# Sums of down weights in DRAM at fixed places of each upper block, and no product of the modulation at the end of a head of the mixer

## The chip, the cores and the metric

The kernel runs on one core of one Trainium2 chip. The metric is the device time in microseconds (us). Everything is computed in one launch; weights and activations are f32 in DRAM, and the matrix products are made of pairs of fp32r numbers.

## What is computed (the reference, cut)

One layer of a residual block for 512 tokens of width 2048. A vector `c` gives six modulation vectors by one product with `w_ada` (12288 x 2048). The block has a mixer (a recurrent group and eight attention heads, both fed by one projection) and a gated feed-forward part of inner width 5632.

```python
mod = silu(c) @ w_ada[l] + b_ada[l]
sh1, sc1, gt1, sh2, sc2, gt2 = split(mod, 6)
h = rms_norm(x, g_mix) * (1 + sc1) + sh1
xr, yr, q, k, v, f_logit = split(h @ w_in, ...)
y_rec = rglru_group(xr, yr, ...)                    # conv, gates, scan, GeLU gate
y_att = forgetting_attention_group(q, k, v, f_logit, ...)   # 8 heads of 128
x = x + gt1 * (concat(rms_norm(y_rec), rms_norm(y_att)) @ w_out)
h2 = rms_norm(x, g_ffn) * (1 + sc2) + sh2
gate, up = split(h2 @ w_up, 2)
x = x + gt2 * ((silu(gate) * up) @ w_down)
```

## The kernel before

**How a product is made.** TensorE (PE) has no f32 product of full speed here, so each operand is split into a high part (ScalarE, ACT, a copy to fp32r) and a low part (VectorE, DVE, the difference), and each tile is multiplied three times: high by high, high by low, low by high (`mm`, L275). Weights are loaded from DRAM by DMAs that SyncE issues (SP queue), split by `wsplit` (L268; the tiles are called `...h` and `...l`), and there are three buffers of each. PE takes a half piece of weights (two k-steps) after another.

**The mixer.** For each head h, `tm_group` (L322) multiplies by the weights of the next head while `attention(h)` (L571) is worked off in hooks: small functions that are traced after a k-step n = 0 to 15 of that product. The statement `head_evac` (L560) copies a finished product out of PSUM at the start of a head, partly on DVE (L565), partly on ACT (L567, L568); the accumulators are used again by the next product. The softmax of a query block ends in a scaling on DVE (L633), then PE transposes (L639). Other hooks carry the recurrent group.

**The products of the modulation ("ada").** `ada_block` (L169) makes one block of 128 rows of `w_ada` times `c`: two DVE instructions on 128x1024 f32 (L178), each on a tile that a DMA brings (L166); the DMA of the next block is issued with the block before it. `ada1` (L509) makes one block; `H_ADA` (L49) says after which k-steps of which head one is made, and `WO_ADA` (L48) the same for the four column groups of the output projection, which come after the mixer. `behind` (L153) adds an order on DVE: not before the last instruction of a list (`norm_last`: the head's query and key normalisation, for steps up to 7; `soft_last`: the last softmax scaling, for later ones).

**The upper half of the feed-forward part.** After two ordinary groups come NBLK = 10 blocks b = 0 to 9. In each, a fast 2x2 scheme makes seven products instead of eight, in the order `ORDER` = 4, 5, 1, 7, 6, 2, 3 (L1145). A block loads four weight units U_A, U_C, U_B, U_D of 2 MB each in four DMAs (`load_unit`, L1150, L1163): U_A and U_C when product 4 is traced, U_B at product 1, U_D at product 2, all with a priority that puts them 2000 places ahead. Sums of units are made on DVE (`sum_unit`, L1168, L1170; two instructions a sum, on 128x2048): A+C for product 5, C+B for product 7, A+B for product 6, A+D for product 3. In between DVE makes pieces of the last modulation vector (`Gt2.piece`, L217, L222) from loads `gt` that SP issues in each block (`Gt2.loads`, L205, L211). Activations of the block before are transposed (`back`, L1196) and stored by eight DMAs `td` (L1088 to L1091).

**The sums of down weights in DRAM.** The lower half needs, for each of NQ = 11 parts q, a sum of three pieces of `w_down` (`s2d`) and of that with a fourth (`s4d`). `sums24(q, n)` makes them without an engine's arithmetic: step n = 0 copies two pieces DRAM to DRAM by four DMAs of 512 KB on the SP queue (L1105, L1106), behind the last weight load traced so far; steps 1 and 2 add two pieces to `s2d`, step 3 adds `s2d` to `s4d`, each by two accumulating DMAs of 512 KB on the queue of GpSimd (POOL, L1098).

```python
def dram_sum(out, src):
    for i in range(2):
        cs = slice(i * 1024, (i + 1) * 1024)
        nc.gpsimd.dma_start(out=out[:, cs], in_=src[:, cs], accum_op=ALU.add)
```

A product has eight k-steps j; after j = 3 and j = 7 a half is counted, so that a block has 14 halves. The counter `halves` runs through all ten blocks: with `SUMS_AT, SUMS_PER = 2, 12` a step n of a part comes every third half, and a new part every 12 halves, so that its place in the block moves from block to block.

**What sets the order.** A scheduler orders the instructions of each engine and queue ahead of time, by the place at which they are traced, by priorities and by `issue_after`; on the chip each engine and queue works its list off in that order and waits for semaphores. SP has the loads, the `td` stores and step 0 of the sums; POOL has in the upper half only the accumulating DMAs.

Of the kernel before, what the change touches and what calls it, by code (L numbers as in the profile page):

```python
# [44 lines left out]
T_STEPS = ((10, 11, 13, 15), (0, 4, 9, 15))  # L45
YR0_AHEAD = 80
CARRY = (0, 0, 1, 1, 1, 3, 3, 6)
WO_ADA = ((8, 10, 12, 14), (0, 3, 6, 9, 12), (0, 3, 6, 9, 12), (0, 3, 6, 9))  # L48
H_ADA = {1: (4, 7, 13, 15), 2: (4, 7, 13, 15), 3: (4, 7, 13, 15), 4: (4, 7, 13), 5: (4, 7, 13),  # L49
         6: (4, 7, 13, 15), 7: (1, 4, 7, 8, 10, 13)}  # L50
BIAS_STEPS = {0: (0, 0, 1, 1, 2, 2, 3, 3, 4, 4, 5, 5, 6, 6, 7, 7, 8, 8, 14, 15),
              1: (0, 0, 1, 1, 2, 2, 3, 3, 4, 4, 5, 5, 6, 6, 7, 7, 12, 13, 13, 14, 14, 14, 15, 15),
              2: (0, 0, 1, 1)}
# [7 lines left out]
KEEP = (2, 8, 2)  # L61
GT2_STEPS = ((4, 1), (4, 2), (4, 3), (4, 5), (4, 7), (5, 5), (6, 1))
GT2_N = (6, 6, 6, 6, 6, 6, 7, 7, 7, 7)
SUMS_AT, SUMS_PER = 2, 12
BU_PART = (0, 5, 10, 16)
BUP_STEP = 3
NQ = FT // 4
# [7 lines left out]
def block_kernel(ctx, tc, xT, crow, adaT, vecs, bfr, w1, wyr, wqkv0, wqkv, wgate, wout, wup0, wups, wdn, outT):  # L75
    nc = tc.nc
# [71 lines left out]
    mods = [cp.tile([P, KT], F32, name=f"mod{j}") for j in range(6)]  # L148

    ada_ready = {}  # L150
    soft_last, norm_last, gated = [], [], []

    def behind(f, gate):  # L153
        def g():
            gated[:] = gate
            f()
            gated.clear()
        return g
# [264 lines left out]
    for kt in range(KT):  # L423
# [12 lines left out]
        h, l = page(f"hph{kt}", "h"), page(f"hpl{kt}", "h")  # L436
# [16 lines left out]
    for f in (4, 5, 6, 7, 0, 1, 2, 3):  # L453
        t = page(f"xr{f}", "c")
# [32 lines left out]
    for kt in range(10):  # L487
        hk0.setdefault(max(RX_STEP, kt * 8 // 5), []).append(lambda kt=kt: sh1_block(kt))
    yr0 = fm_group(wyr[0], list(range(KT)), hp, "yr0", hooks=hk0, ahead=YR0_AHEAD,
                   ps=[misc(f"yr0p{f}") for f in range(3)] + [rgp("yr0p3")])  # L490
    rstd_x = rx[0]
    yr = []
    for f in range(4):
        t = page(f"yr{f}", "c")
# [10 lines left out]
    def add(hooks, n, *fns):  # L505
        hooks.setdefault(n, []).extend(fns)
        return hooks
# [52 lines left out]
    def head_evac(h, ps):  # L560
        qk = qp.tile([P, NT, 2 * P], F32, tag="qk", name=f"qk{h}")
        v = page(f"v{h}", "d", [P, NT, P])
        for t in range(NT):
            if t % 2:
                nc.vector.tensor_copy(out=qk[:, t, :], in_=ps[t][:, 0:256])  # L565
            else:
                nc.scalar.activation(qk[:, t, :], ps[t][:, 0:256], AF.Copy)  # L567
            nc.scalar.activation(v[:, t, :], ps[t][:, 256:384], AF.Copy)  # L568
        return qk[:, :, 0:P], qk[:, :, P:2 * P], v
# [266 lines left out]
    ps = tm_group(wqkv0, hs_, "h0", 392, hooks=hk0)  # L836
    frest = None
    for h in range(NH):
        with tc.high_priority(offset=EVAC):
            ev = head_evac(h, ps)  # L840
        if h == 0:
            frest = forget(ps)
            make_spn()
            conv_sums()
        att = attention(h, *ev)
        att[0]()
        hk = {}
        for n, f in zip(CARRY, carry):
            add(hk, n, f)
        carry = []  # L850
        if h == 0:
            for n, f in zip(FORGET_STEPS, frest):
                add(hk, n, f)
        for n, f in zip((FIRST_STEPS if h == 0 else ATT_STEPS if h < NH - 1 else LAST_STEPS)[1:], att[1:]):
            add(hk, n, f)
        for n in BIAS_STEPS.get(h, ()):
            f = lambda: bias_in(len(bias_done))
            add(hk, n, behind(f, soft_last) if h or n > 11 else f)
        if h == 2:
            add(hk, 2, bias_sum)  # L860
        if 2 <= h < 6:
            rp = rec_pair((2 * h - 4, 2 * h - 3))
            for n, f in zip(REC_STEPS, rp):
                add(hk, n, f)
            carry = rp[len(REC_STEPS):]
        for n in H_ADA.get(h, ()):
            add(hk, n, behind(ada1, soft_last if n > 7 else norm_last) if h < 7 else ada1)
        if h < NH - 1:
            ps = tm_group(wqkv[h], hs_, f"h{h + 1}", 384, hooks=hk)
    att_rms = cp.tile([P, NT], F32, name="att_rms")  # L870
# [119 lines left out]
    for g in range(4):  # L990
        hk = {}
# [15 lines left out]
        for f in range(4):  # L1007
            kt = g * 4 + f
            t = page(f"x1_{kt}", "c")
# [90 lines left out]
    def sums24(q, n):  # L1100
        if n == 0:
            with tc.issue_after((up_loads or stream_loads)[-1]):
                for i in range(2):
                    cs = slice(i * 1024, (i + 1) * 1024)
                    nc.sync.dma_start(out=s2d[q][:, cs], in_=wdn[0, q, :, cs])  # L1105
                    nc.sync.dma_start(out=s4d[q][:, cs], in_=wdn[1, q, :, cs])  # L1106
        elif n < 3:
            dram_sum(s2d[q], wdn[n + 1, q])
        else:
            dram_sum(s4d[q], s2d[q])  # L1110
# [11 lines left out]
    for gi in range(STD):  # L1122
        hk = {}
# [80 lines left out]

    gt2_left = [(r, i) for r in range(4) for i in range(KT)]
    hk = {}
    nprod = halves = 0
    for b in range(NBLK):
        un, keep_ = {}, {}
        gt2 = Gt2(gt2_left[:GT2_N[b]])  # L1210
# [4 lines left out]
        for i, p in enumerate(ORDER):  # L1215
# [3 lines left out]
            for j, hi, lo in prod_weights(p, b, un):  # L1219
                th, tl = T[p][j]  # L1220
                for t in range(2):
                    c_ = slice(t * P, (t + 1) * P)
                    mm(ps[t], th[:, c_], hi, j == 0, False)
                    mm(ps[t], th[:, c_], lo, False, False)
                    mm(ps[t], tl[:, c_], hi, False, j == 7)
                for fn in hk.get((i, j), ()):
                    fn()
                if j % 4 == 3:
                    n = halves - SUMS_AT
                    halves += 1  # L1230
                    if 0 <= n < SUMS_PER * NQ and n % SUMS_PER % 3 == 0 and n % SUMS_PER < 12:
                        sums24(n // SUMS_PER, n % SUMS_PER // 3)
            if b + i == 0:
                up_last()
            if p in (4, 5, 1, 7):
# [259 lines left out]
```

## Time and profile before

| | us |
|---|---|
| median of 3 runs | 2028.64 |
| lowest and highest of them | 2025.68, 2032.72 |
| the profiled execution, its own time | 2028.19 |
| its span in the profile | 2026.5 |
| PE busy, of that span | 2005.5 |
| DVE busy | 1678.2 |
| ACT busy | 986.8 |

The page gives, for each engine, the time in which it has an instruction at work, and for each group of instructions the idle time before it and what ended that idle time (the releaser). A stretch (window) gives the same for a part of the span, with the clock granted to PE as a share of full speed and the mean busy share of the 16 DMA engines; a share a little over 1 comes from rounding. Times in the text are us from the start of the span; "into the block" means from the first matmul of product 4 of that block. The ten blocks begin at 813.7, 889.8, 968.0, 1046.4, 1131.7, 1209.8, 1288.0, 1366.1, 1444.2 and 1522.4.

### The profile page before, as it was taken

What the parts mean: (1) busy time and instruction counts of PE and PEld (TensorE: products, weight loads), DVE (VectorE), ACT (ScalarE), POOL (GpSimd) and SP (SyncE); (2) the same over time, 40 slices, a digit from 0 to 9 for tenths busy, and PEclk for the clock granted to TensorE, in tenths of its full rate; (3) what the DMA queues carried; (4) which work ended last, traced back from release to release, by engine and by line L of the source; (5) the groups of instructions that cost most, each with busy time, mean ns of one, the idle gap of its engine ahead of it and who ended that gap; (6) DMA issues with size and microseconds to landing.
All of it is one profiled execution on the core that took longest, in us unless ns stands there. A gap on an engine that the chain in (4) does not pass through costs nothing.

```text
span 2026.5 us, 25606 instructions
## 1 busy us (share of the span) xinstructions
PE 2005.5 (99%) x9330; PEld 1688.7 (83%) x9330; DVE 1678.2 (83%) x2300; ACT 986.8 (49%) x1362; POOL 109.8 (5%) x138
## 2 busy tenths in 40 slices
PE   9999999999999999999999999999999999999999
PEld 7889988898888888888887888888888888888887
DVE  8999788877787769898797888988988977777786
ACT  4433446775422257544544544445445455445443
POOL 0000100111000000000010000000000100000000
PEclk9999999999999999999999999999999999999999
DMA  9989866557679874779698868878696677778793
GB/s 354 346 296 336 281 213 209 199 170 258 225 256 319 327 259 143 184 201 270 187 280 236 207 235 228 208 261 238 187 289 186 222 249 245 253 239 295 257 331 119
DMA packets 173683, 496.33 MB, mean 245 GB/s; under 512 B 18434, under 2 KB 41138, under 8 KB 169459
## 3 DMA queue, kind: packets, MB, share of 16 engines
q1 hardware_dynamic: 162372, 454.99, 65.4%
q0 software_dynamic: 11040, 39.59, 11.2%
q8 instruction: 73, 1.20, 0.2%
q14 instruction: 54, 0.44, 0.1%
q10 hardware_dynamic: 144, 0.11, 0.0%
HBM read 458.93 MB, written 93.36 MB: 273 GB/s over the span
## 4 chain that ended last, share of the span: by engine, by line
PE 87%; DVE 6%; issue 4%; DMA 2%; ACT 1%; POOL 0%; DVEq 0%; POOLq 0%; ACTq 0%
PE up_2p L276 5%; PE up_6p L276 5%; PE up_3p L276 5%; PE up_5p L276 5%; PE up_1p L276 5%; PE up_7p L276 5%; PE up_4p L276 5%; PE w1p L276 4%; PE dn4p L276 3%; PE dn6p L276 3%; PE dn3p L276 3%; PE dn1p L276 3%; PE dn2p L276 3%; PE dn7p L276 3%; PE dn5p L276 3%
## 5 line engine op out<-in xcount | busy, mean ns | idle before, releaser
L1170 DVE TENSOR_TENSOR uw<-uw,uw 128x2048 f32<-128x2048 f32 x80 | 182.5, 2282 | 2.0 <-DMA uw<-in_wups 2.0
L178 DVE SCALAR_TENSOR_TENSOR ada<-ada,c_b 128x1024 f32<-128x1024 f32 x96 | 116.7, 1221 | 46.3 <-DMA ada<-in_adaT 46.1
L271 ACT ACTIVATE up_1h<-uw 128x1024 fp32r<-128x1024 f32 x70 | 74.4, 1063 | 118.9 <-PE up_6p L276 21.6
L271 ACT ACTIVATE up_0h<-uw 128x1024 fp32r<-128x1024 f32 x70 | 74.3, 1062 | 115.0 <-PE up_4p L276 16.6
L272 DVE TENSOR_TENSOR up_1l<-uw,up_1h 128x1024 fp32r<-128x1024 f32 x70 | 85.3, 1219 | 36.1 <-ACT up_1h L271 36.1
L272 DVE TENSOR_TENSOR up_0l<-uw,up_0h 128x1024 fp32r<-128x1024 f32 x70 | 85.4, 1220 | 33.6 <-ACT up_0h L271 33.5
L271 ACT ACTIVATE up_3h<-uw 128x1024 fp32r<-128x1024 f32 x70 | 74.4, 1063 | 71.7 <-PE up_2p L276 14.9
L271 ACT ACTIVATE up_2h<-uw 128x1024 fp32r<-128x1024 f32 x70 | 74.2, 1060 | 58.4 <-PE up_2p L276 16.5
L272 DVE TENSOR_TENSOR up_2l<-uw,up_2h 128x1024 fp32r<-128x1024 f32 x70 | 85.3, 1218 | 20.0 <-ACT up_2h L271 19.9
L272 DVE TENSOR_TENSOR up_3l<-uw,up_3h 128x1024 fp32r<-128x1024 f32 x70 | 85.2, 1217 | 10.3 <-ACT up_3h L271 10.3
L1098 POOL DMA_DIRECT2D s2d<-in_wdn x44 | 36.5, 842 | 624.2 <-DMA s2d<-in_wdn 624.2
L276 PE MATMUL w1p<-hph,w1l 128*128 128x512 f32 x128 | 49.8, 389 | 0.0
L276 PE MATMUL w1p<-hpl,w1h 128*128 128x512 f32 x128 | 49.8, 389 | 0.0
L222 DVE SCALAR_TENSOR_TENSOR gt<-gt,gt_None 128x512 f32<-128x512 f32 x64 | 43.0, 683 | 5.5 <-DMA gt<-in_adaT 5.5
L276 PE MATMUL w1p<-hph,w1h 128*128 128x512 f32 x128 | 42.6, 392 | 0.0
L188 DVE SCALAR_TENSOR_TENSOR ada<-ada,c_b 128x1024 f32<-128x1024 f32 x32 | 39.0, 1218 | 4.0 <-DMA ada<-in_adaT 4.0
L188 DVE SCALAR_TENSOR_TENSOR adf<-adf,c_b 128x1024 f32<-128x1024 f32 x32 | 39.0, 1219 | 0.3 <-DMA adf<-in_adaT 0.3
L631 ACT ACTIVATE bt<-bt,nm 128x128 f32<-128x128 f32 (+3 forms) x32 | 17.9, 561 | 34.8 <-DVE nm L629 34.5
L712 DVE SCALAR_TENSOR_TENSOR ba<-bw,sh,ba 128x512 f32<-128x512 f32 x45 | 32.2, 743 | 0.0
L616 POOL TENSOR_SCALAR_AFFINE_SELECT bt<-bt 128x128 f32<-128x128 f32 x32 | 22.8, 735 | 116.2 <-ACT bt L615 116.2
L437 ACT ACTIVATE hph<-x,A 128x512 fp32r<-128x512 f32 x16 | 11.6, 723 | 35.0 <-DVE A L434 35.0
L276 PEld LDWEIGHTS w1p<-hph,w1h 128*128 128x128 f32 x128 | 24.0, 188 | 5.4 <-issue 0.6
(2293 smaller groups left out, 6637.8 us busy)
## 6 DMA issues: line engine op xcount, KB each, us to landing
uw<-in_wups SPq DMA_DIRECT2D x160, 512.0 KB, 7.2
ada<-in_adaT SPq DMA_DIRECT2D x128, 512.0 KB, 5.4
s2d<-in_wdn POOLq DMA_DIRECT2D x44, 512.0 KB, 8.8
adf<-in_adaT SPq DMA_DIRECT2D x32, 512.0 KB, 6.0
gt<-in_adaT SPq DMA_DIRECT2D x64, 256.0 KB, 6.1
s2d<-in_wdn SPq DMA_DIRECT2D x22, 512.0 KB, 8.9
s4d<-in_wdn SPq DMA_DIRECT2D x22, 512.0 KB, 9.9
s4d<-s2d POOLq DMA_DIRECT2D x22, 512.0 KB, 8.2
```

Source lines behind the costliest of these rows:

```text
L178: nc.vector.scalar_tensor_tensor(out=t, in0=t, scalar=1.0, in1=cs, op0=ALU.mult, op1=ALU.mult, accum_out=ac)
L188: nc.vector.scalar_tensor_tensor(out=t, in0=t, scalar=1.0, in1=c_b[:, cs], op0=ALU.mult, op1=ALU.mult, accum_out=ada_acc[j][:, hf, i:i + 1])
L222: nc.vector.scalar_tensor_tensor(out=t, in0=t, scalar=1.0, in1=c, op0=ALU.mult, op1=ALU.mult, accum_out=gt2_acc[:, r, i:i + 1])
L271: tail_hi.append(nc.scalar.activation(R(hi[:, :n]), raw_ap, AF.Copy).ins)
L272: tail_lo.append(nc.vector.tensor_sub(R(lo[:, :n]), raw_ap, hi[:, :n]).ins)
L276: nc.tensor.matmul(ps, lhsT=R(l), rhs=R(r), start=start, stop=stop)
L437: nc.scalar.activation(R(h), xt, AF.Copy, scale=a)
L616: nc.gpsimd.affine_select(out=bt[:, b * P:n], in_=bt[:, b * P:n], pattern=[[-1, P]], compare_op=ALU.is_ge, fill=NEG, base=0, channel_multi ...
L631: nc.scalar.activation(p[:, :n], p[:, :n], AF.Exp, scale=-1.0, bias=nm, accum_out=sm)
L712: nc.vector.scalar_tensor_tensor(out=ba[j], in0=src, scalar=s1, in1=ba[j], op0=ALU.mult, op1=ALU.add)
L1098: nc.gpsimd.dma_start(out=out[:, cs], in_=src[:, cs], accum_op=ALU.add)
L1170: nc.vector.tensor_add(d_, d_, s_)
```

## The change

1. **Sums.** The running counter goes. In blocks 0 to 8 step 0, 1, 2, 3 of part q = b are traced at half 1, 3, 9, 12 of the block. In block 9 part 9 is traced at halves 0, 2, 4, 6 and part 10 at halves 7, 9, 11, 13. The functions that make the sums are as before.
2. **Products of the modulation.** In heads 1, 2, 3 and 6 there is no longer one after k-step 15. In heads 2, 3 and 6 there is one after k-step 1 instead, in head 1 none; the first group of the output projection has five (steps 7, 9, 11, 13, 14) in place of four (8, 10, 12, 14).
3. **Order.** A product at a step up to 2 is put behind a new list, `evac_last`: the last DVE copy of the head's evacuation (L565).

```diff
-WO_ADA = ((8, 10, 12, 14), (0, 3, 6, 9, 12), (0, 3, 6, 9, 12), (0, 3, 6, 9))
-H_ADA = {1: (4, 7, 13, 15), 2: (4, 7, 13, 15), 3: (4, 7, 13, 15), 4: (4, 7, 13), 5: (4, 7, 13),
-         6: (4, 7, 13, 15), 7: (1, 4, 7, 8, 10, 13)}
+WO_ADA = ((7, 9, 11, 13, 14), (0, 3, 6, 9, 12), (0, 3, 6, 9, 12), (0, 3, 6, 9))
+H_ADA = {1: (4, 7, 13), 2: (1, 4, 7, 13), 3: (1, 4, 7, 13), 4: (4, 7, 13), 5: (4, 7, 13),
+         6: (1, 4, 7, 13), 7: (1, 4, 7, 8, 10, 13)}
-SUMS_AT, SUMS_PER = 2, 12
+SUMS_STEPS = {1: 0, 3: 1, 9: 2, 12: 3}
+SUMS_LAST = {0: (9, 0), 2: (9, 1), 4: (9, 2), 6: (9, 3), 7: (10, 0), 9: (10, 1), 11: (10, 2), 13: (10, 3)}
-                nc.vector.tensor_copy(out=qk[:, t, :], in_=ps[t][:, 0:256])
+                evac_last[:] = [nc.vector.tensor_copy(out=qk[:, t, :], in_=ps[t][:, 0:256]).ins]
-            add(hk, n, behind(ada1, soft_last if n > 7 else norm_last) if h < 7 else ada1)
+            add(hk, n, behind(ada1, soft_last if n > 7 else norm_last if n > 2 else evac_last) if h < 7 else ada1)
-                    n = halves - SUMS_AT
-                    halves += 1
-                    if 0 <= n < SUMS_PER * NQ and n % SUMS_PER % 3 == 0 and n % SUMS_PER < 12:
-                        sums24(n // SUMS_PER, n % SUMS_PER // 3)
+                    n = 2 * i + j // 4
+                    if b < NBLK - 1 and n in SUMS_STEPS:
+                        sums24(b, SUMS_STEPS[n])
+                    elif b == NBLK - 1 and n in SUMS_LAST:
+                        sums24(*SUMS_LAST[n])
```

More of the change, by code (lines that the diff above doesn't have):

```diff
@@ L150, in block_kernel @@
     ada_ready = {}
-    soft_last, norm_last, gated = [], [], []
+    soft_last, norm_last, evac_last, gated = [], [], [], []
     def behind(f, gate):
@@ L1206, in block_kernel @@
     hk = {}
-    nprod = halves = 0
+    nprod = 0
     for b in range(NBLK):
```

## The prediction

> **What bounds the kernel now.** I read the page first, then the waits of PE, then stretches of one block each, then the order in time of DVE, SP and POOL around the one block that differs. The page's first lines:
>
> ```profile
> span 2026.5 us, 25606 instructions
> PE 2005.5 (99%) x9330; PEld 1688.7 (83%) x9330; DVE 1678.2 (83%) x2300; ACT 986.8 (49%) x1362; POOL 109.8 (5%) x138
> ```
>
> PE is the bound, and the change takes no matmul away. All it can win is idle time of PE, 2026.5 - 2005.5 = 21.0 us, and what a slower clock adds. The waits of PE (us in total, times, longest):
>
> ```profile
> PE pt L639 <- DVE bt L633: 4.0, 3, 1.6
> PE up_6p L276 <- DVE up_2l L272: 3.6, 1, 3.6
> PE h3p L276 <- ACT v L568: 1.7, 2, 1.1
> PE h5p L276 <- ACT v L568: 1.7, 1, 1.7
> PE h0p L276 <- ACT hh L478: 1.4, 1, 1.4
> PE up_6p L276 <- DVE up_1l L272: 1.3, 1, 1.3
> ```
>
> The two `up_6p` rows lie in product 6 of one block; `h3p` and `h5p` are the first matmuls of the products that start heads 2 and 4 and wait until the accumulators of the product before are copied out; `pt` is the softmax's end. Stretches of one block each (us, busy time of PE, PEld, DVE, ACT, POOL, granted clock, DMA share, GB/s), blocks 3, 7 and 9, and a piece of block 3:
>
> ```profile
> 1046.40:1131.70 85.30, 80.42 (x354) 65.57 (x353) 67.73 (x75) 38.19 (x44) 6.57 (x8) 0.98 0.86 236
> 1366.10:1444.20 78.10, 78.10 (x353) 64.56 (x352) 68.12 (x78) 38.21 (x44) 8.22 (x10) 1.00 0.93 256
> 1522.40:1600.60 78.20, 78.20 (x354) 64.61 (x353) 68.83 (x79) 39.26 (x46) 0.81 (x1) 1.00 0.63 202
> 1104.00:1110.00 6.00, 6.00 (x21) 4.76 (x20) 6.00 (x7) 1.06 (x1) 0.00 (x0) 0.72 0.25 98
> ```
>
> Block 3 takes 85.3 - 78.2 = 7.1 us more: 3.6 + 1.3 = 4.9 us of waits, and 2.2 us of slower matmuls after them, where the granted clock is 0.72. Blocks 7 and 9 have PE busy throughout.
>
> **Why block 3 waits.** DVE, in order of time:
>
> ```profile
> 1094.43 0.69 DVE L222 SCALAR_TENSOR_TENSOR gt<-gt,gt_None 128x512 f32<-128x512 f32 x1 [5.46 <-DMA gt<-in_adaT]
> ...
> 1099.46 2.29 DVE L1170 TENSOR_TENSOR uw<-uw,uw 128x2048 f32<-128x2048 f32 x1 [1.96 <-DMA uw<-in_wups]
> 1101.67 1.22 DVE L272 TENSOR_TENSOR up_2l<-uw,up_2h 128x1024 fp32r<-128x1024 f32 x1
> ```
>
> The sum A+D for product 3 stands on DVE ahead of `up_2l` of product 6. It waited for U_D, which landed 1099.46 - 1046.4 = 53.1 us into the block, and a `gt` piece ahead of it waited until 48.0. Both are late DMAs. SP and POOL in block 3:
>
> ```profile
> 1042.17 0.50 SPq L1105 DMA_DIRECT2D s2d<-in_wdn  x1
> ...
> 1077.52 8.35 SPq L211 DMA_DIRECT2D gt<-in_adaT  x5
> 1086.00 11.21 SPq L1163 DMA_DIRECT2D uw<-in_wups  x8
> ```
>
> ```profile
> 1051.47 0.82 POOL L1098 DMA_DIRECT2D s4d<-s2d  x1 [3.35 <-DMA s2d<-in_wdn]
> 1059.47 0.81 POOL L1098 DMA_DIRECT2D s2d<-in_wdn  x1 [7.17 <-DMA s2d<-in_wdn]
> ...
> 1082.23 0.81 POOL L1098 DMA_DIRECT2D s4d<-s2d  x1 [4.67 <-DMA s2d<-in_wdn]
> ```
>
> Step 0 of part 4 goes out at 1042.17, when part 3 still has accumulates to make (its last at 1051.47); part 4's six follow from 13.1 to 35.8 us into the block and meet `gt` (from 31.1) and U_D (from 39.6). In the stretch 1040 to 1100 the two queues (packets, MB, share of all DMA engines) and the times to landing were:
>
> ```profile
> q0 software_dynamic: 1441, 5.24, 53.9%
> q1 hardware_dynamic: 4546, 9.84, 46.6%
> ...
> s4d<-s2d POOLq DMA_DIRECT2D x4, 512.0 KB, 10.7
> gt<-in_adaT SPq DMA_DIRECT2D x6, 256.0 KB, 13.2
> ```
>
> POOL's 5.24 MB hold the DMA engines for longer than SP's 9.84. So two parts' sums in close succession cost block 3 its 7.1 us. POOL's rows also show what paces them: every accumulate is released by a landing, none by PE or DVE. The places of steps 1, 2, 3 set only POOL's order, which stays; what moves is step 0.
>
> **Where step 0 goes.** It stands right behind the last weight load traced. For half 1 that is U_C of the same block, which SP issues in the block before. Part 8 is traced at such a place now: it begins at half 2 + 8 x 12 = 98 of the count, which is half 0 of block 7 (98 = 7 x 14). SP and POOL then:
>
> ```profile
> 1350.81 0.56 SPq L1105 DMA_DIRECT2D s2d<-in_wdn  x1
> ```
>
> ```profile
> 1376.89 0.81 POOL L1098 DMA_DIRECT2D s4d<-s2d  x1 [6.67 <-DMA s2d<-in_wdn]
> 1379.37 0.84 POOL L1098 DMA_DIRECT2D s2d<-in_wdn  x1 [1.67 <-DMA s2d<-in_wdn]
> 1388.27 0.82 POOL L1098 DMA_DIRECT2D s4d<-s2d  x1 [8.05 <-DMA s2d<-in_wdn]
> ```
>
> It starts 1366.1 - 1350.81 = 15.3 us before block 7; its last accumulate is issued 22.2 us into it, ahead of `gt` at 31. Block 7 loses nothing. After the change parts 0 to 8 all lie so, 78 us apart: term 1 is **-7.1 us** in block 3. This step costs nothing elsewhere as long as a burst is over before `gt`; the cover is 31.1 - 22.2 = 8.9 us from last issue to `gt`'s issue.
>
> **Block 9 now has two parts.** Part 9 (half 0) goes behind U_C(9), 15.3 us before the block. Part 10 (half 7) goes behind U_B(9): part 4 begins at half 2 + 48 = 50, half 8 of block 3, also behind U_B, and its step 0 was issued 1046.4 - 1042.17 = 4.2 us before that block. So the two parts start 15.3 - 4.2 = 11 us apart. What is queued behind them on SP are `td`, `gt` and U_D(9); on POOL, part 10's accumulates stand behind part 9's, and in block 9 nothing else. Block 9 before:
>
> ```profile
> 1553.27 2.98 SPq L211 DMA_DIRECT2D gt<-in_adaT  x5
> ```
>
> ```profile
> 1568.85 2.29 DVE L1170 TENSOR_TENSOR uw<-uw,uw 128x2048 f32<-128x2048 f32 x1
> ```
>
> `gt` goes out 30.9 us into the block, U_D behind it, and A+D runs at 46.5 without a wait. Part 10's first accumulate can go out between the last two issues of part 9, by part 8's rows 13.3 us (1379.37 - 1366.1) and 22.2 us (1388.27) into the block. From first to last issue part 4 took 1082.23 - 1059.47 = 22.8 us, and the last `s4d` 10.7 more to land: part 4 was done 35.8 + 10.7 = 46.5 us into block 3, part 10 will be 46.8 to 55.7 into block 9. `gt` came to DVE at 48.0 in block 3, when POOL was done, and U_D 5 us behind it; so in block 9 U_D comes 0.3 to 9.2 us later than there. I take 2.5, nearer the early end, since POOL's queue is seen to interleave pieces (an `s2d` at 1379.37 behind an `s4d` at 1376.89). Term 2 is **+9.6 us** (7.1 + 2.5). Its bounds: 0, if U_D lands in time; and 7.1 + 9.2 + 8.2 = 24.5, if part 10's own four loads also delay part 9's chain, by 2.1 MB at block 7's 256 GB/s = 8.2 us.
>
> The Trainium skill, page "DMA: Bandwidth & Descriptors", section "Queues, rings and completion order", has a DMA engine go round the queues that hold work, one packet at a time. By that rule `gt` and U_D crawl for as long as POOL has packets queued, term 2 cannot be 0, and the sum would lie between 2028.19 - 10.5 + 7.4 = 2025.1 and 2034.0; the shares above (1441 packets holding 53.9%) agree with it.
>
> **The mixer.** The end of head 3 on DVE:
>
> ```profile
> 353.96 1.23 DVE L178 SCALAR_TENSOR_TENSOR ada<-ada,c_b 128x1024 f32<-128x1024 f32 x1 [1.64 <-DMA ada<-in_adaT]
> ...
> 355.11 0.75 DVE L565 COPY qk<-h4p 128x256 f32<-128x256 f32 x2
> ```
>
> The product after step 15 holds DVE, partly waiting for its own DMA, and head 4's evacuation copies stand behind it; PE waits 1.7 us (`h5p`), in head 2 likewise 1.7 (`h3p`). Heads 5 and 6, entered without such a product, show no such wait (heads 3 and 7, entered with one, show none either), so both go: term 3 is **-3.4 us**. Heads 2, 3 and 6 get 2 x 1.23 = 2.5 us of DVE after step 1, behind the evacuation; the DMAs of the next block move with it. What is behind it on DVE is the query and key normalisation, and later the softmax. Head 3, and the output projection's first group with its added product:
>
> ```profile
> 308.70:353.50 44.80, 43.37 (x238) 39.46 (x236) 38.49 (x72) 33.57 (x57) 4.31 (x5) 1.00 0.62 205
> 537.80:586.30 48.50, 48.29 (x226) 39.35 (x225) 42.13 (x67) 21.07 (x31) 2.92 (x2) 1.00 0.71 245
> ```
>
> DVE has 44.8 - 38.49 = 6.3 us free in head 3 and 6.4 in the projection's group, which hide it; if that cover is gone, it costs up to 2.5 each in head 3 and in the projection. On the other side the three `pt` waits (4.0) could shrink. I take 0 for this.
>
> **Sum** against the profiled execution, 2028.19 us (1.7 over its span, 0.45 under the median of 2028.64): -7.1 + 9.6 - 3.4 = -0.9, so **2027.3 us**.
>
> **Rivals.** (a) *Part 10 is harmless in block 9*: block 9's DMA share before is 0.63 against 0.86, with no weights for a next block. Term 2 is 0: 2028.19 - 10.5 = 2017.7. It decides if POOL is done before `gt` needs the engines; against it, the chain's end as worked out lies past A+D's 46.5 in every case, so part 10 would have to run faster than part 4. Chance 0.32. (b) *Slower: the second burst waits for all of the first*, the late bound, term 2 = 24.5: 2028.19 - 10.5 + 24.5 = 2042.2. Slower by more than 0.3% begins where term 2 passes 16.6. For it: POOL works in order. Against: block 9 is quieter. Chance 0.12. (c) *The mixer gives its gain back*: the product after step 1 delays the softmax, so 3.4 + 2 x 2.5 us come back: 2027.3 + 8.4 = 2035.7. Chance 0.05. (d) *The change doesn't space the sums*, as POOL paces itself: that is true of steps 1 to 3 and is in the forecast.
>
> **How the numbers follow.** 0.3% of 2028.64 is 6.1 us, about what this measurement can tell from no change. The forecast, term 2 from 6 to 14, gives 2023.7 to 2031.7, all within it, chance 0.51. Faster: rival (a), 0.32, and 0.01 from a mixer that gains more. Slower: (b) and (c) less what of them stays within, 0.16. The range takes in (a) down to 2016.5 and (b) up to term 2 = 18, 2035.7.
>
> **What would show it.** Blocks 1 to 8 at 78.2 us, block 3 without `up_6p` waits; step 0 of part 10 on SP at some 4 us before block 9; block 9 at 84 to 92 us with DVE L1170 waiting for `uw<-in_wups` and a stretch of lowered clock behind it; no wait of `h3p` and `h5p` for `v`. Wrong: block 9 at 78.2, or a wait in another block, or part 10's step 0 elsewhere on SP.

## The result, and the profile after

The changed kernel takes 2048.09 us (median of 4 runs, 2043.8 to 2051.05); the kernel before took 2028.47 beside it (2025.68 to 2032.72). The ratio is 1.0091, with a 95% interval of 1.0076 to 1.0106. The prediction was 2027.3 with a range of 2016.5 to 2035.7, so it was wrong: the change costs 0.9%. The profiled execution took 2047.83 us. The head of its page:

```profile
span 2046.1 us, 25606 instructions
PE 2012.7 (98%) x9330; PEld 1692.2 (83%) x9330; DVE 1678.1 (82%) x2300; ACT 986.5 (48%) x1362; POOL 109.8 (5%) x138
```

The span grew by 19.6 us. PE's idle time went from 21.0 to 2046.1 - 2012.7 = 33.4 us, which is 12.4 of it; the other 7.2 are the same matmuls taking longer. Line numbers of the changed kernel are one higher than before (L276 is now L277); in some of the runs below they are higher by up to three more. The waits of PE (us in total, times, longest):

```profile
PE up_6p L277 <- DVE up_2l L273: 5.7, 1, 5.7
PE up0p L277 <- ACT hrh L932: 5.6, 1, 5.6
PE up_6p L277 <- DVE up_1l L273: 5.0, 1, 5.0
PE pt L640 <- DVE bt L634: 4.5, 5, 1.8
...
PE h3p L277 <- ACT v L569: 1.0, 2, 0.8
PE yr1p L277 <- ACT v L569: 0.9, 1, 0.9
PE qkt L595 <- DVE qk L587: 0.9, 1, 0.9
```

The wait of `h5p` is gone, as forecast. That of `h3p`, which was to go too, is 1.0 us (1.7 before). The two `up_6p` waits are still there, and larger. A wait of `up0p`, the first matmul after the output projection, is new. Stretches of the changed kernel (columns as before: busy time of PE, PEld, DVE, ACT, POOL, granted clock, DMA share, GB/s): block 3, block 9, two pieces of block 9, and the start of `up0`:

```profile
1057.00:1135.10 78.10, 78.10 (x353) 64.57 (x352) 67.44 (x75) 38.21 (x44) 4.95 (x6) 1.00 0.81 223
1525.90:1620.20 94.30, 83.62 (x354) 67.81 (x353) 69.33 (x79) 39.13 (x46) 9.10 (x11) 0.93 0.90 241
1578.70:1585.50 6.80, 5.49 (x12) 3.80 (x12) 2.10 (x5) 0.00 (x0) 0.00 (x0) 0.50 1.05 332
1589.00:1595.80 6.80, 5.13 (x12) 4.07 (x13) 6.80 (x9) 0.03 (x1) 0.00 (x0) 0.50 0.86 338
...
729.00:735.60 6.60, 6.07 (x14) 4.41 (x14) 6.47 (x10) 4.49 (x7) 0.00 (x0) 0.50 0.91 252
```

Block 3 is at 78.1 us (85.3 before). Block 9 takes 94.3 us in place of 78.2. Of the 16.1 us, 5.0 + 5.7 are waits. The other 5.4 are slower matmuls (83.62 us of PE busy in place of 78.20): two stretches of 6.8 us are at half clock. Each of them begins shortly before the end of its wait, so that PE is busy for 5.49 and 5.13 us of it. So the waits moved from block 3 to block 9 and grew. The rest is ahead of the blocks: `up0` starts at 729.5 in place of 722.1, block 0 at 824.2 in place of 813.7. The account in the span: +10.5 ahead of block 0, -7.1 in block 3, +16.1 in block 9, which makes 19.5.

**Block 9.** DVE of the changed kernel, in order of time (start, duration, instruction, idle time before it and its releaser):

```profile
1577.57 0.69 DVE L223 SCALAR_TENSOR_TENSOR gt<-gt,gt_None 128x512 f32<-128x512 f32 x1 [9.09 <-DMA gt<-in_adaT]
...
1578.19 1.22 DVE L273 TENSOR_TENSOR up_1l<-uw,up_1h 128x1024 fp32r<-128x1024 f32 x1
...
1587.19 2.29 DVE L1171 TENSOR_TENSOR uw<-uw,uw 128x2048 f32<-128x2048 f32 x1 [5.71 <-DMA uw<-in_wups]
```

SP and POOL in the same block:

```profile
1521.80 0.60 SPq L1106 DMA_DIRECT2D s2d<-in_wdn  x1
...
1572.84 4.99 SPq L1164 DMA_DIRECT2D uw<-in_wups  x4
```

```profile
1543.58 1.66 POOL L1099 DMA_DIRECT2D s2d<-in_wdn  x2 [1.93 <-DMA s2d<-in_wdn]
1554.11 0.83 POOL L1099 DMA_DIRECT2D s4d<-s2d  x1 [8.88 <-DMA s2d<-in_wdn]
...
1577.67 0.81 POOL L1099 DMA_DIRECT2D s4d<-s2d  x1 [5.23 <-issue]
```

Part 10's step 0 goes out at 1521.80, 4.1 us before the block, as worked out. Its first accumulate is the second of the two from 1543.58 on, 18.3 us into the block and ahead of part 9's last one (1554.11), as worked out too. Its last goes out at 1577.67, which is 51.8 us into the block, so that from its first to its last accumulate it takes 33.5 us; `gt` comes to DVE at 51.7 (48.0 in block 3 before) and the sum A+D runs at 61.3 (53.1 there). The chain of the forecast holds link by link; it only takes longer than I took it to.

**The start of `up0`.** `hrh` is a scaling by `a2`, and `a2` comes from the modulation vector sc2, whose products of `ada` are the last ones. DVE before:

```profile
699.62 1.22 DVE L178 SCALAR_TENSOR_TENSOR ada<-ada,c_b 128x1024 f32<-128x1024 f32 x1
...
706.28 1.22 DVE L178 SCALAR_TENSOR_TENSOR ada<-ada,c_b 128x1024 f32<-128x1024 f32 x1
...
713.96 1.23 DVE L178 SCALAR_TENSOR_TENSOR ada<-ada,c_b 128x1024 f32<-128x1024 f32 x1 [2.19 <-DMA ada<-in_adaT]
...
717.92 0.17 DVE L925 SCALAR_TENSOR_TENSOR a<-mod,vec 128x16 f32<-128x16 f32 x1
```

and after:

```profile
702.05 1.23 DVE L179 SCALAR_TENSOR_TENSOR ada<-ada,c_b 128x1024 f32<-128x1024 f32 x1
...
712.32 1.42 DVE L955 SCALAR_TENSOR_TENSOR x<-x,mod,x 128x512 f32<-128x512 f32 x2 [5.31 <-DMA x<-in_xT]
...
716.88 1.22 DVE L179 SCALAR_TENSOR_TENSOR ada<-ada,c_b 128x1024 f32<-128x1024 f32 x1
...
724.59 1.23 DVE L179 SCALAR_TENSOR_TENSOR ada<-ada,c_b 128x1024 f32<-128x1024 f32 x1 [4.20 <-DMA ada<-in_adaT]
...
728.54 0.17 DVE L926 SCALAR_TENSOR_TENSOR a<-mod,vec 128x16 f32<-128x16 f32 x1
```

The third product from the end is late by 702.05 - 699.62 = 2.4 us, the last but one by 716.88 - 706.28 = 10.6, and so is `a2`. In between stands an `x` instruction (`x1_fin`, L955, the residual's addition) that waited 5.31 us for its DMA. SP after:

```profile
702.08 1.56 SPq L167 DMA_DIRECT2D ada<-in_adaT  x2
704.45 0.33 SPq L283 DMA_DIRECT2D up0r<-in_wup  x1
704.84 1.41 SPq L407 DMA_DIRECT2D x<-in_xT  x2
...
718.14 2.01 SPq L167 DMA_DIRECT2D ada<-in_adaT  x2
```

and before:

```profile
693.22 0.33 SPq L406 DMA_DIRECT2D x<-in_xT  x1
...
699.64 1.57 SPq L166 DMA_DIRECT2D ada<-in_adaT  x2
```

Before, the last `x` load of `x1_fin` (693.22) went out ahead of the `ada` load; after, two go out behind it, and behind `up0r` (704.84). The last `ada` load (718.14) goes out right when the product before it (716.88 + 1.22) has freed its buffer, and comes 6.5 us later. So the products here form a chain of product, load, next product. Counted from the start of the output projection to `a2`, this chain has 20 products before and 21 in the changed kernel; before, it takes 717.9 - 537.8 = 180 us, 9 us a product.

**The mixer.** The product `h6p` starts at 397.6 (400.6 before), so 3.0 us were won by then; 2.5 are left where the last mixer product starts (`yr1p`, 484.3 against 486.8), and that product takes 53.4 us in place of 51.0, with the new waits `yr1p` and `qkt`. The projection's first group, with its fifth product, takes 50.1 us in place of 48.5. So the second group starts 1.5 us later than before (587.8 against 586.3).

### The profile page after: what moved, and what is told of

It reads as the page before. It is cut to its first block, busy times and chain, and to the rows that moved or that the text cites. A ratio compares the mean times of both kernels' runs of the same rounds, so it can differ in the third digit from the quotient of the medians.

```text
span 2046.1 us, 25606 instructions
## 1 busy us (share of the span) xinstructions
PE 2012.7 (98%) x9330; PEld 1692.2 (83%) x9330; DVE 1678.1 (82%) x2300; ACT 986.5 (48%) x1362; POOL 109.8 (5%) x138
## 3 DMA queue, kind: packets, MB, share of 16 engines
q0 software_dynamic: 11040, 39.59, 11.6%
## 4 chain that ended last, share of the span: by engine, by line
PE 77%; issue 9%; DMA 6%; DVE 6%; POOL 1%; ACT 1%; SPq 0%; DVEq 0%; POOLq 0%; ACTq 0%
PE up_2p L277 5%; PE up_6p L277 5%; PE up_3p L277 5%; PE up_5p L277 5%; PE up_1p L277 5%; PE up_7p L277 5%; PE up_4p L277 5%; PE w1p L277 4%; PE dn4p L277 3%; PE dn6p L277 3%; PE dn3p L277 3%; PE dn1p L277 3%; PE dn2p L277 3%; PE dn5p L277 3%; PE dn7p L277 3%
## 5 line engine op out<-in xcount | busy, mean ns | idle before, releaser
L272 ACT ACTIVATE up_0h<-uw 128x1024 fp32r<-128x1024 f32 x70 | 74.3, 1062 | 122.0 <-PE up_4p L277 16.6
L273 DVE TENSOR_TENSOR up_0l<-uw,up_0h 128x1024 fp32r<-128x1024 f32 x70 | 85.5, 1222 | 33.5 <-ACT up_0h L272 33.4
L273 DVE TENSOR_TENSOR up_3l<-uw,up_3h 128x1024 fp32r<-128x1024 f32 x70 | 85.3, 1219 | 10.3 <-ACT up_3h L272 10.3
L277 PE MATMUL w1p<-hpl,w1h 128*128 128x512 f32 x128 | 49.8, 389 | 0.0
L277 PE MATMUL w1p<-hph,w1l 128*128 128x512 f32 x128 | 49.8, 389 | 0.0
L277 PE MATMUL w1p<-hph,w1h 128*128 128x512 f32 x128 | 42.6, 392 | 0.0
L713 DVE SCALAR_TENSOR_TENSOR ba<-bw,sh,ba 128x512 f32<-128x512 f32 x45 | 32.2, 745 | 0.0
L978 DVE SCALAR_TENSOR_TENSOR bu_acc<-bu,mod,bu_acc 128x512 f32<-128x512 f32 x30 | 22.5, 749 | 9.0 <-DMA bu<-in_wup 8.6
L438 ACT ACTIVATE hph<-x,A 128x512 fp32r<-128x512 f32 x16 | 11.6, 724 | 36.7 <-DVE A L435 36.7
```

What stands on the lines that cost most here:

```text
L272: tail_hi.append(nc.scalar.activation(R(hi[:, :n]), raw_ap, AF.Copy).ins)
L273: tail_lo.append(nc.vector.tensor_sub(R(lo[:, :n]), raw_ap, hi[:, :n]).ins)
L277: nc.tensor.matmul(ps, lhsT=R(l), rhs=R(r), start=start, stop=stop)
L713: nc.vector.scalar_tensor_tensor(out=ba[j], in0=src, scalar=s1, in1=ba[j], op0=ALU.mult, op1=ALU.add)
L978: nc.vector.scalar_tensor_tensor(out=a, in0=src, scalar=s2, in1=a, op0=ALU.mult, op1=ALU.add)
```

## The experiments

The table has all of them: medians, the ratio to the kernel before on the same chip with its interval, and from the profile the start of block 0, the lengths of blocks 3 and 9, and that of the down projection up to PE's end (us).

| run | median | ratio | block 0 at | block 3 | block 9 | down |
|---|---|---|---|---|---|---|
| before | 2028.5 | | 813.7 | 85.2 | 78.2 | 421.1 |
| after | 2048.1 | 1.0091 (1.0076 to 1.0106) | 824.2 | 78.1 | 94.3 | 421.1 |
| e1 sums only | 2035.7 | 1.0043 (1.0026 to 1.0060) | 813.5 | 78.1 | 92.9 | 421.1 |
| e2 ada only | 2034.5 | 1.0032 (1.0019 to 1.0045) | 824.7 | 82.1 | 78.2 | 421.1 |
| e3 part 10 behind U_D | 2035.6 | 1.0036 (1.0023 to 1.0048) | 823.2 | 78.1 | 78.1 | 427.8 |
| e4 x loads earlier | 2044.0 | 1.0077 (1.0062 to 1.0092) | 823.4 | 78.1 | 93.5 | 421.1 |
| e5 part 10 in down | 2031.5 | 1.0019 (1.0009 to 1.0028) | 817.2 | 78.1 | 78.2 | 431.4 |
| e6 = e5 + product in projection | 2041.2 | 1.0058 (1.0040 to 1.0076) | 827.4 | 78.1 | 78.2 | 430.3 |
| e7 = e5 + heads 2, 3, 6 | 2030.0 | 1.0006 (0.9997 to 1.0016) | 812.5 | 78.1 | 78.2 | 430.3 |
| e8 = e7 + product in head 4 | 2029.1 | 1.0003 (0.9993 to 1.0013) | 812.3 | 78.1 | 78.1 | 430.6 |
| e9 = e8, part 0 before blocks | 2021.3 | 0.9970 (0.9959 to 0.9982) | 812.7 | 78.1 | 78.2 | 421.1 |
| e10 five products earlier | 2042.8 | 1.0076 (1.0060 to 1.0091) | 820.3 | 78.1 | 93.6 | 421.1 |
| e11 parts 9, 10 apart | 2031.4, one run | | 822.5 | 78.1 | 79.6 | 421.1 |
| e12 part 10 loads only | 2027.8, one run | | 820.4 | 78.1 | 78.2 | 421.1 |
| e13 x and bu loads earlier | 2043.7 | 1.0068 (1.0047 to 1.0089) | 821.4 | 78.1 | 93.4 | 421.1 |
| e14 e9's sums alone | 2024.8 | 0.9976 (0.9966 to 0.9987) | 819.2 | 78.1 | 78.1 | 421.1 |
| e15 product more in head 5 | 2036.5 | 1.0042 (1.0025 to 1.0059) | 813.3 | 78.1 | 94.2 | 421.1 |

Before, e1, e5 and e14 have every product at its old place and no sums ahead of the second ordinary group of the upper half. Yet their profiled executions start the output projection between 537.7 and 539.7 and block 0 between 813.5 and 819.2. So a single start of block 0 is good to some 6 us, and where it matters the medians are compared as well.

### The two parts of the change alone

e1 takes the new `SUMS_STEPS` and `SUMS_LAST` and keeps the old product places; e2 takes the new places and keeps the counter of halves.

> Only the fixed places of the DRAM sums; the ada products stay where they were before. Theory: the 19.6 us are three separate sums, 10.5 up to the start of block 0 (from the ada part), -7.1 in block 3 and +16.1 in block 9 (from the sums). Then this kernel is -7.1 + 16.1 = 9.0 us slower than before, about 2037.5, with block 0 starting at 814, block 3 at 78 us and block 9 at 94 us. Rival: block 9's loss needs the shifted tail of the ada part as well; then block 9 is at its 78 us and the time is about 2021.

> Only the moved ada products; the sums stay counted in halves as before. Theory: the loss ahead of block 0 comes from this part alone, 10.5 us, about 2039, with a wait of some 5.6 us for hrh ahead of up0 and a stretch of half clock behind it, and with block 3's wait of 7 us still there. Rival: the mixer's forecast gain holds by itself (-3.4, about 2025), and the loss ahead of up0 needs the sums' change too.

e1: 2035.7, block 0 at 813.5, block 3 at 78.1, block 9 at 92.9. Its rival falls: block 9's loss is the sums' alone. e2: block 0 at 824.7, with a `up0p` wait of 5.2 us; the loss ahead of block 0 is the ada part's alone, and its rival falls. e2 is faster than expected in part since block 3 lost 3.9 us there and not 7. e1 is 8.3 us slower than the runs of before beside it and e2 7.1. Both have won in block 3 (e1 7.1 us, e2 3.1), and that can be had only once. So the 3.1 of e2 come on top of the two losses: 8.3 + 7.1 + 3.1 = 18.5, against 2048.1 - 2028.5 = 19.6 for the whole change.

### Where part 10 goes

```diff
-..., 7: (10, 0), 9: (10, 1), 11: (10, 2), 13: (10, 3)}
+..., 10: (10, 0), 11: (10, 1), 12: (10, 2), 13: (10, 3)}   # e3
```

> The changed kernel with the steps of part 10 at halves 10, 11, 12 and 13 of block 9 in place of 7, 9, 11 and 13, so that its first step goes out behind the last weight load of block 9 (U_D) and no longer ahead of that block. Theory: block 9's 16.1 us come from part 10's transfers lying ahead of and among block 9's weight loads; they go, and the time is 2048.1 - 16.1 = 2032, block 9 at 78 to 79 us. Rival: the bytes are what is short, wherever they lie within this stretch; the down projection's first loads then wait instead, its span grows by 10 us or more and the time stays near 2048.

Block 9 is at 78.1 us, so its 16 us came from part 10. But 6.7 us come back in the down projection, whose second product starts 19.3 us after its first in place of 12.7; PE's new wait there:

```profile
PE up_t L1200 <- DVE uu L1264: 3.2, 1, 3.2
```

The theory is right on the cause, the rival on part of the bytes. e5 moves part 10 further, into the first phase of the down projection, and has all products at their old places:

```diff
+SUMS_DOWN = {6: 0, 7: 1, 8: 2, 9: 3}
                 dn_open(ph, q)
+                if ph == 0 and q in SUMS_DOWN:
+                    sums24(10, SUMS_DOWN[q], dn_loads[-1])
```

> Ada products as before; the sums of parts 0 to 9 at fixed places, one part to a block, and part 10 moved out of the blocks into the first phase of the down projection (its four steps at quarters 6 to 9 of that phase), 60 us and more behind the last block's loads. Theory: fixed places win block 3's 7.1 us, and part 10 costs nothing where the load is lighter: 2028 - 7 = 2021, all blocks near 78.2 us, the down projection at its 421 us. Rival: the DMA engines have no room for part 10 in the down projection either, as with part 10 right behind the last weight load, where that stage grew by 6.7 us; then 2028.

The rival holds: that stage grows by 10.3 us, more than in e3.

```profile
PE dn4p L278 <- ACT dq_6w0h L273: 5.0, 1, 5.0
```

The product waits for the weights of its seventh quarter; part 10's four loads and six accumulates run just then (from 1633.4 to 1684.2) and are what is new there. This stage, with a DMA share of about 0.7 before, had no room for one part at this place. Two more runs take the mechanism in block 9 apart. e12 leaves part 10's accumulates out and keeps its loads; e11 sets the parts at the distance of parts 3 and 4 before:

```diff
-SUMS_LAST = {0: (9, 0), 2: (9, 1), ..., 7: (10, 0), ...}
+SUMS_LAST = {0: (9, 0), 2: (9, 1), 4: (9, 2), 6: (9, 3), 7: (10, 0)}   # e12
+SUMS_LAST = {2: (9, 2), 5: (9, 3), 8: (10, 0), 10: (10, 1), 12: (10, 2), 13: (10, 3)}   # e11, with
+SUMS_8 = {10: (9, 0), 13: (9, 1)}   # in block 8
```

> The changed kernel with the accumulates of part 10 left out (its steps 1 to 3; the part is loaded and not summed), so that only its four loads of 512 KB lie ahead of block 9. Theory: the accumulates hold the DMA engines, the loads cost little: block 9 at 78 to 80 us. Rival: part 10's loads delay part 9's accumulates and the weights by themselves, 2.1 MB at 256 GB/s = 8 us; then block 9 stays at 84 us or more.

> The changed kernel with parts 9 and 10 as far apart as parts 3 and 4 were before: part 9 from half 10 of block 8 (steps 0 and 1 there, 2 and 3 at halves 2 and 5 of block 9), part 10 from half 8 of block 9. Theory: the loss of block 9 goes by the distance of the two first steps; at the distance of parts 3 and 4 it is what block 3 lost, 7 us, in place of 16: block 9 at 85 us, 2039. Rival: block 9's loss comes from having the end of the loads and part 10 together, whatever part 9 does; then block 9 stays at 92 to 94 us.

e12's block 9 and e11's:

```profile
1522.00:1600.20 78.20, 78.20 (x354) 64.61 (x353) 68.83 (x79) 39.27 (x46) 4.12 (x5) 1.00 0.86 249
```

```profile
1523.90:1603.50 79.60, 78.74 (x353) 64.49 (x352) 68.69 (x79) 39.44 (x46) 5.72 (x7) 1.00 0.90 263
```

Without the accumulates PE is busy all through: part 10's 2.1 MB of loads alone cost nothing, and the loss needs its accumulates. With the parts 27.2 us apart (27.6 between parts 3 and 4 before, 11.2 in the changed kernel) 1.4 of the 16 us are left, less than the 7 that I expected from block 3, which also carries the loads of a following block. Part 10's accumulates on POOL in e11, the first and the last:

```profile
1535.79 0.83 POOL L1100 DMA_DIRECT2D s2d<-in_wdn  x1 [9.41 <-DMA s2d<-in_wdn]
...
1556.10 0.81 POOL L1100 DMA_DIRECT2D s4d<-s2d  x1 [3.02 <-DMA s2d<-in_wdn]
```

Part 9's last one went out at 1525.56, so the two bursts of accumulates no longer overlap on POOL. Part 10's now takes 20.3 us and not 33.5, its last goes out 32.2 us into the block and not 51.8, and A+D runs at 48.9 us and not at 61.3. So the distance of the two parts decides, and at equal distance block 9 lost less than block 3. Both runs are of one execution each, but what they lose in block 9 is far from 16 us.

### What makes `a2` late

```diff
-        xt = load_x(kt, "x3_")
+        with tc.high_priority(offset=60):
+            xt = load_x(kt, "x3_")        # e4; e13 the same for the bu load too
```

> The changed kernel with the x loads of the output projection's close (x1_fin) given a little more priority, so that x_10 stands again ahead of the loads of ada_13 and x_11 ahead of those of ada_14 on SP. Nothing else is edited. Theory: the late x loads hold up the x1 lines on VectorE, these the last ada products, these a2 and hrh; the 5.6 us wait ahead of up0 and the half clock behind it go, about 9 us, to 2039. Rival: the fifth product in the projection's first group is simply one more product of VectorE time on the way to a2, and the place of the x loads only goes along with it; then nothing or at most 1 to 2 us is won, 2046 to 2048.

My theory failed: the wait of `up0p` is 5.5 us as before, and block 0 starts at 823.4. The `x` loads are early now, and the last load of `up_bias` took their place in DVE's order (waits of DVE in the last group):

```profile
DVE bu_acc L979 <- DMA bu<-in_wup: 8.4, 2, 5.1
```

Which step brings it on was the next question. e6 and e7 stand on e5, with its extra 10 us in the down projection:

```diff
-WO_ADA = ((8, 10, 12, 14), ...)          # e6: this and head 1 alone
+WO_ADA = ((7, 9, 11, 13, 14), ...)
-H_ADA = {1: (4, 7, 13, 15), 2: (4, 7, 13, 15), 3: (4, 7, 13, 15), ...   # e7: heads 2, 3, 6 alone
+H_ADA = {1: (4, 7, 13, 15), 2: (1, 4, 7, 13), 3: (1, 4, 7, 13), ...
+H_ADA = {1: (4, 7, 13), 2: (1, 4, 7, 13), 3: (1, 4, 7, 13), 4: (1, 4, 7, 13), ...   # e8
```

> As the kernel with part 10 in the down projection, and of the ada part only this: the product that ended head 1 is moved into the output projection's first group as its fifth. Theory: this step alone makes the loss ahead of block 0. With it the shift by SH2 is ready some 2.5 us later, the bias products of up (bu) start some 5 us later, and every later load on SP that waits for VectorE comes later in turn, until a2 is some 9 us late: up0 waits 5 to 6 us for hrh and runs at half clock behind it, 2030 to 2032 against 2021. Rival: the moved products of heads 2, 3 and 6 are needed for it; then there is no such wait and the time is that of the kernel without this step.

> As the kernel with part 10 in the down projection, and of the ada part only this: the products at the end of heads 2, 3 and 6 go behind the copies after step 1 of the next head. Theory: no wait of up0 for hrh; the waits of h5p and part of h3p for v go, and what of that is kept at the start of the output projection is between 0 and 3.4 us: 2018 to 2021. Rival: these moves bring on the loss ahead of up0; then up0 waits and the time is 2030.

> As the kernel with part 10 in the down projection, with the whole ada part of the change but one place: head 1's product goes to step 1 of head 4 in place of the output projection's first group. No head ends with a product and the first group has its four. Theory: the wait of up0 is gone, the start of block 0 is as before or up to 3 us earlier: 2018 to 2022. Rival: one product more or less in the first group is not what matters, but any change of the products' order against the projection's loads; then up0 waits and the time is about 2030.

The step is settled: with the one product moved into the projection (e6) `up0p` waits 5.7 us, and block 0 starts 10.2 us later than in e5; the medians differ by 9.7. With the other moves (e7), or with that product in head 4 (e8), there is no such wait. Against e5, e7 and e8 are 1.6 and 2.5 us faster by the medians, with intervals that overlap. All four carry part 10's 10 us in the down projection, which the numbers expected of them did not have.

What of the fifth product does it? e10 keeps five products, each one or two steps earlier, e13 moves both kinds of load, e15 has one product more ahead of the projection:

```diff
-WO_ADA = ((7, 9, 11, 13, 14), ...)
+WO_ADA = ((5, 7, 9, 11, 13), ...)        # e10
-         ... 5: (4, 7, 13),
+         ... 5: (1, 4, 7, 13),           # e15
```

> The changed kernel with the five products of the output projection's first group behind its steps 5, 7, 9, 11 and 13 in place of 7, 9, 11, 13 and 14. Five products as before, the last one a step earlier. Theory: what matters is when the last of them makes the shift by SH2 ready, since the bias products of up start on it; some 2 us earlier there, the later loads keep their order, the wait of up0 for hrh shrinks by most of its 5.6 us and the half clock behind it goes: block 0 starts at 815 to 817, 2048 - 8 = 2040. Rival: five products cost VectorE too much in that group wherever they stand; then block 0 starts at 823 or later, 2047 or more.

> The changed kernel with a little more priority for the x loads and also for the bu loads of the output projection, so that all 16 bu loads and x_11 go out on SP ahead of the loads of ada_14 (with the x loads alone, the last bu load still stood behind them and behind up0r, and VectorE waited 5.1 us for it). Theory: whichever load VectorE needs ahead of the last two ada products and SP issues behind ada_14 and up0r holds up a2; with none there, the last product's load goes out some 5 to 6 us earlier, the wait of up0 for hrh is under 1 us and the half clock is gone: block 0 starts at 815 to 818, 2040 to 2042. Rival: the lag of the bias products from the start of the projection is the cause, whatever the order of the last loads; then up0 still waits 4 us and more and block 0 starts at 822 or later, 2047.

> The changed kernel with one ada product more ahead of the output projection, at step 1 of head 5; the projection's own places stay, so that one product is left for its end in place of two. Theory, after the misses with the loads' order: what comes late is the end of one serial chain, product, then the load into its buffers (7 to 8 us), then the next product, up to a2; a load or bias product that stands ahead of a link in VectorE's order only shifts it. With one link fewer at the end a2 is ready some 8 us sooner, ahead of the end of the projection's matmuls; the wait of up0 for hrh goes, block 0 starts at 813 to 817 and the time is 2038 to 2041. Rival: VectorE as such is overloaded from the mixer's end on (more work ahead of the projection makes the projection later); then the product in head 5 comes back as a longer mixer and block 0 still starts at 822 or later.

e10: half. The wait falls to 2.5 us, block 0 starts at 820.3; DVE again waits 7.0 us for the last `bu` load ahead of the last but one product. e13: the wait of `up0p` for `hrh` is gone, and yet `a2` is ready at 728.2 as in the changed kernel, `up0` starts at 729.1, and the projection's last group itself now waits 3.0 us for its weights. What I gave that load I took from others on the same queue. Neither theory had all of it right: the order of these loads decides where the lag shows, not whether there is one. e15 settles it. DVE in e15 at the end of the projection:

```profile
707.30 1.54 DVE L978 SCALAR_TENSOR_TENSOR bu_acc<-bu,mod,bu_acc 128x512 f32<-128x512 f32 x2 [6.04 <-DMA bu<-in_wup]
...
711.03 1.22 DVE L179 SCALAR_TENSOR_TENSOR ada<-ada,c_b 128x1024 f32<-128x1024 f32 x1
...
712.72 0.18 DVE L926 SCALAR_TENSOR_TENSOR a<-mod,vec 128x16 f32<-128x16 f32 x1
```

DVE waits for the same late `bu` load, 6.04 us, and it does no harm: the chain has one link fewer from the projection's start on, 20, `a2` is ready at 712.7, 8.5 us before `up0` (721.2) starts, and block 0 starts at 813.3. The time is 2036.5, 11.6 under the changed kernel, though DVE makes one product more ahead of the projection: the rival, a shortage of DVE's time, falls. All runs fall into two groups by this count: with 20 products `a2` comes 177 to 185 us after the start of the projection (before, e1, e5, e7 to e9, e14, e15), with 21 it comes after 187 to 192 (the changed kernel and its other variants).

### A version that beats both

e9 is e8 with the sums one block earlier throughout, part 0 in the second ordinary group of the upper half (`up1`, 769 to 813), so that no block has two parts and none is left over. e14 is the same with all products at their old places.

```diff
+SUMS_UP1 = ((0, 0), (4, 1), (8, 2), (12, 3))
+        if gi == 1:
+            for at, n in SUMS_UP1:
+                add(hk, at, lambda n=n: sums24(0, n))
...
+                    if n in SUMS_STEPS:
+                        sums24(b + 1, SUMS_STEPS[n])
```

> The ada places of the kernel with head 1's product in head 4, and the sums at fixed places one block earlier throughout: part 0 in the second standard up product (up1), parts 1 to 10 in blocks 0 to 9. No two parts start less than a block apart and none is left for the down projection. Theory: block 3's 7.1 us stay won, block 9 stays at 78.2 us, the down projection at 421 us, and the kernel is faster than both: 2028 - 7 - 1.5 = 2019 to 2020. Rival: part 0 in up1 meets the loads of block 0 and of up1 and makes PE wait there; then 5 us and more come back, 2025.

> The sums one block earlier throughout (part 0 in up1, parts 1 to 10 in blocks 0 to 9) with every ada product where it was before. Theory: what the kernel with both parts won, 5.3 us, is block 3's 7.1 us less 2 us in block 0, and the moved ada products give at most 2 us of it: 2021 to 2023, block 0 at 78.3 us. Rival: most of it comes from the ada part; then 2026 or more.

e9 takes 2021.25 us (2019.62 to 2023.12), a ratio of 0.9970 (0.9959 to 0.9982), 0.3% faster than before; e14 0.9976 (0.9966 to 0.9987). The head of e9's page:

```profile
span 2020.6 us, 25603 instructions
PE 2004.6 (99%) x9330; PEld 1688.8 (84%) x9330; DVE 1677.6 (83%) x2300; ACT 986.3 (49%) x1362; POOL 108.4 (5%) x138
```

PE's idle time is 16.0 us (21.0 before). Blocks 3 and 9 and the down projection are undisturbed; block 0 gives 2.1 us back (78.3 in place of 76.2, with two new waits of 1.3 and 0.3 us). Parts 0 and 1 start 55 us apart there and not 78; whether that brings on these waits was not tried. The two intervals overlap, so most of the gain is the sums', and what the moved products add is not settled.

## Why the prediction was wrong

1. **Block 3, -7.1: right.** 85.2 to 78.1 us in the changed kernel and in every run with fixed places.
2. **Block 9, +9.6: the mechanism right, the size wrong.** It measured +16.1 (14.7 in e1). The prediction said that U_D would come "0.3 to 9.2 us later than there. I take 2.5, nearer the early end, since POOL's queue is seen to interleave pieces". The A+D sum ran at 61.3 us into the block, 8.2 later than in block 3; 7.1 + 8.2 = 15.3 is nearly what was measured, and the late end of that span, 7.1 + 9.2 = 16.3, still nearer. POOL did interleave, yet part 10 was not done sooner for it. The term that was too small is the length of part 10's chain: the prediction took over the 22.8 us from first to last issue of part 4, and beside part 9's last accumulates it was 33.5 (20.3 in e11, where the two don't overlap). The queues of block 9 (packets, MB, share of all DMA engines from 1525.9 to 1603.9):

```profile
q1 hardware_dynamic: 5659, 12.80, 48.2%
q0 software_dynamic: 1586, 5.77, 45.7%
```

   POOL's 1586 packets hold the engines for 78 x 16 x 0.457 / 1586 = 0.36 us each, of 5.77 MB / 1586 = 3.6 KB; SP's for 78 x 16 x 0.482 / 5659 = 0.11, of 2.3 KB. That is twice the time for a byte. From the Trainium skill's rule (page "DMA: Bandwidth & Descriptors", section "Queues, rings and completion order": queues are served in turn, a packet at a time) the prediction had concluded that this term can't be 0. The 16.1 us of block 9 agree with that; no run here shows the turns themselves. e12 shows that the loss needs the accumulates.
3. **The mixer, -3.4: nearly right where it was forecast, and lost behind it.** By `h6p` the change had won 3.0 us, though `h3p` kept 1.0 us of its wait (kernels with all products at their old places start `h6p` between 399.9 and 402.2, so 3.0 is little more than the scatter); 2.5 were left at `yr1p`, whose product then took 2.4 more. In e8, without the fifth product in the projection, the second group starts at 583.5 (586.3 before), near the forecast, but with the 2 us of scatter this isn't settled.
4. **The product moved into the projection, 0: wrong, and the largest miss.** The step that failed is: "DVE has 44.8 - 38.49 = 6.3 us free in head 3 and 6.4 in the projection's group, which hide it; if that cover is gone, it costs up to 2.5 each". In that group itself the fifth product cost 1.6 us (50.1 against 48.5), within the bound. The rest came behind it. Of the 10.5 us ahead of block 0, 1.6 were there at the start of the projection's last group (678.4 against 676.8), 5.8 came at `up0` and 3.1 at half clock behind it; alone, in e6, the step cost 10.2 (9.7 by the medians). Free time of DVE in the group was the wrong cover to name. The moved product is not 2.5 us of work that finds a gap; it is one link of a serial chain (product, load, product) that has to end before `up0`. The slack was in the rows of before: `a2` at 717.92, `up0` at 722.1, so 4.2 us. A link late by 10.6 us goes past that by 6.4. The rival (c), a mixer that gives its gain back, had a price of 8.4 us, near this, and the wrong place.
5. **Rivals.** (a), part 10 harmless, had the highest chance of them and was wrong: the worked-out end of POOL's chain spoke against it, and I gave it a third all the same. (b), slower by the late bound of block 9, names the right place. Its condition did not come, since part 10 did not wait for all of part 9; its size of 24.5 was too large, the 16.1 measured fall just short of its decision point of 16.6, and the projection's 10.5 came on top.

The range left the projection out, for which the text had named a bound of 2.5 us that was itself too small. With the sums alone (e1) the time, 2035.7, would have stood at its upper end.

## What to carry to other kernels

When work is moved to where an engine is free, ask first what the moved work feeds: follow its result to the matmul that needs it, read the slack there, and count the loads that stand behind it on the queue. Where two bursts of DMA meet, read how far apart they start and which of them accumulate, since in this kernel that decided; find each burst a place of its own, ahead of the stage if need be, and don't take a stage's mean DMA share for room. Where a term is worked out between two bounds, don't take the early one for want of a reason against it.

## What was not expected of the hardware

A PE wait costs more than itself. With each of the waits of 5.0, 5.7 and 5.6 us came 6.6 to 6.8 us at a granted clock of 0.50, which cost 5.4 us for the first two together and 3.1 for the third. It does not take so long a wait: in e10 2.5 us of wait ahead of `up0` were followed by a stretch of lower clock, and at its end the clock was full again:

```profile
727.80:731.20 3.40, 3.40 (x11) 2.66 (x10) 3.40 (x5) 2.58 (x5) 0.00 (x0) 0.56 0.95 273
731.20:734.60 3.40, 3.40 (x16) 2.81 (x15) 2.26 (x4) 0.47 (x1) 0.00 (x0) 1.00 0.99 384
```

The Trainium skill, page "TensorE: Matmul & The Clock Gate", Part 1, gives a window of about 3.4 us for the fall to half speed and for the way back. The length of these stretches agrees, one or two such windows. But the fall came here after less idle time than that: behind 2.5 us of wait in e10, 2.3 in e2 (`up_6p`) and 2.1 in e14 (`wo3p`), each followed by 3.4 us at 0.51 to 0.56.

An accumulating DMA from DRAM to DRAM lands about as soon as a plain one; what makes it dear here is the delay of the loads beside it. No run separates the adding from the queue of POOL, which has no plain copies in the upper half. From the list of DMA issues of the changed kernel (count, size of one, median us to landing), and from that of block 9:

```profile
uw<-in_wups SPq DMA_DIRECT2D x160, 512.0 KB, 6.9
...
s2d<-in_wdn POOLq DMA_DIRECT2D x44, 512.0 KB, 8.8
...
s2d<-in_wdn SPq DMA_DIRECT2D x22, 512.0 KB, 8.5
```

```profile
uw<-in_wups SPq DMA_DIRECT2D x4, 512.0 KB, 13.3
```

The weights of U_D took 13.3 us in place of 6.9. The mean DMA share does not tell such a stage from a harmless one: the changed kernel's block 9 loses 16 us at 0.90, that of e11 1.4 us at 0.90, and block 7 before has no wait at 0.93.
